# Shifting the split weight pieces of an fp32 transformer block off their 256-byte grid

## The chip, the cores and the metric

The kernel runs on one core of one Trainium2 chip, in one launch. The metric is device time in microseconds. The engines have the names of the profile: PE (TensorE: matmuls, with PEld for its weight loads), DVE (VectorE), ACT (ScalarE), POOL (GpSimd), SP (SyncE, which here only issues DMAs).

## What is computed

Two layers of a block with an attention and mLSTM mixer and a convolutional feed-forward part, on 512 positions of width 1024, all in fp32. Cut to what the change touches, which are the products with weights:

```python
D_MODEL, SEQ, DEPTH, D_FF = 1024, 512, 2, 2816

def hybrid_mixer(hn, w_in, ..., w_out):
    aq, ak, av, mq, mk, mv, mo, gates = jnp.split(hn @ w_in, split_at, axis=-1)   # 1024 x 3600
    ...                                     # dilated attention, mLSTM in both directions
    return jnp.concatenate([attn, mlstm], axis=-1) @ w_out                        # 1024 x 1024

def conv_ffn(hn, w_up, conv_w, conv_b, w_down):
    u = depthwise_conv_centred(hn @ w_up, conv_w, conv_b)                         # 1024 x 5632
    gate, val = jnp.split(u, 2, axis=-1)
    return (jax.nn.gelu(gate, approximate=True) * val) @ w_down                   # 2816 x 1024

def reference(x, ...):
    for l in range(DEPTH):
        mixed = hybrid_mixer(rms_norm(x, mix_pre_g[l]), w_in[l], ..., w_out[l])
        x = x + rms_norm(mixed, mix_post_g[l])
        ff = conv_ffn(rms_norm(x, ffn_pre_g[l]), w_up[l], ffn_conv_w[l], ffn_conv_b[l], w_down[l])
        x = x + rms_norm(ff, ffn_post_g[l])
    return x
```

## The kernel before

Activations lie with features on the 128 partitions and the 512 positions along the row. To keep fp32 accuracy on PE, each fp32 operand is split into a high part in PE's fp32r format and the rest, also in fp32r; a product is then three matmuls that add up in PSUM: high weight by high activation (line 224), low weight by high activation (225), high weight by low activation (226). The helper `mac` issues these three for one block of 128 features.

The weights stream from HBM in 208 pieces in a fixed order (`plan`): per layer 28 of w_in, 8 of w_out, 44 of w_up and 24 of w_down. A piece has up to 8 blocks of 128x128, 4096 bytes a partition. `load_raw` brings a piece into one of three buffers `wraw`. `split_w` makes the two parts: ACT copies it to fp32r into `whi` (line 177), and DVE subtracts that from the raw piece into `wlo` (line 115, in `lo_part`). `whi` and `wlo` have three buffers each (RING), so pieces are split ahead, by `prefetch`, as soon as PE has finished with a buffer. 192 of the 208 pieces go there. The other 16 are put by `alloc` into space that other tiles have left (names `wsp`, `wnx`, `wlh`, `wll`, and some `pth`, `ptl`).

For most products a block of a piece is the stationary operand of a matmul and the activation streams past it, 512 columns at a time, or 256 at the edges of a stage. A full piece is then 24 matmuls of 512 columns. In the V projections (two pieces for each of four head groups and layer, lines 920 to 922) it is the other way round: the activation is stationary and 256 columns of a piece stream. In `first_group` and at the start of w_out several pieces are used in turn, block by block. The attention and mLSTM work of the mixer is issued between the steps of its projections, so small matmuls stand among the large ones there; in the feed-forward part, after its first group, hardly anything does.

All tiles of a partition's memory come from a wrapper, `Lines`, that rounds sizes up to 256 bytes; tiles under that size go to a pool of their own. So every large tile begins at a multiple of 256 bytes, and so do the blocks of a piece, 512 bytes each. An exception is in the borrowed space of w_out's third output tile, whose low parts lie in rows of 129 numbers (516 bytes), because the tiles `cs0` and `cs1` whose space it takes are so shaped:

```python
spare = [("kw0", "cs0", 3, 1), ("kw1", "cs1", 3, 1), ("lu", "ut", 1, 2), ("lu", "uu", 1, 2)]
...
w = P + 1 if t[0] == "c" else P
ts.append(mp.tile([P, n * w], F32R, tag=t, ...).rearrange("p (n m) -> p n m", n=n)[:, :, 0:P])
```

The first three blocks of that piece are in kw0 and cs0, the next three in kw1 and cs1. Another is the table tb, whose parts begin 56 bytes behind a multiple of 256.

Of the kernel before, what the change touches and what calls it, by code (L numbers as in the profile page):

```python
# [9 lines left out]
F32R = mybir.dt.float32r  # L10
# [6 lines left out]
P = 128  # L17
# [64 lines left out]
def tile_hybrid_block(ctx: ExitStack, tc: tile.TileContext, xt, w_in, w_g, w_out, w_up, w_down, par, cst, out):  # L82
# [8 lines left out]
    wraw_p, whi_p, wlo_p = Lines(big, small, RAW), Lines(big, small, RING), Lines(big, small, RING)  # L91
# [22 lines left out]
    def lo_part(dst, src, hi):  # L114
        nc.vector.tensor_tensor(out=dst, in0=src, in1=f32v(hi), op=ALU.subtract)  # L115
# [34 lines left out]
    nxt = [0, 0]  # L150

    def load_raw():
        i = nxt[0]
        if i >= len(plan):
            return
        nxt[0] += 1
        nk = plan[i].shape[1]
        raw = wraw_p.tile([P, 8, P], F32, tag="wraw", name="wraw")
        nc.sync.dma_start(out=raw[:, 0:nk, :], in_=plan[i])
        raw_q.append((raw, nk))  # L160

    def split_w(alloc=None):

        if not raw_q:
            return None
        raw, nk = raw_q.popleft()
        parts = {}
        n = 8
        k = 0
        while k < nk:  # L170
            if alloc is None:
                hi = whi_p.tile([P, 8, P], F32R, tag="whi", name="whi")
                lo = wlo_p.tile([P, 8, P], F32R, tag="wlo", name="wlo")
            else:
                hi, lo, n = alloc()
            m = min(n, nk - k)
            nc.scalar.copy(out=hi[:, 0:m, :], in_=raw[:, k:k + m, :])  # L177
            lo_part(lo[:, 0:m, :], raw[:, k:k + m, :], hi[:, 0:m, :])
            for j in range(m):
                parts[k + j] = (hi[:, j, :], lo[:, j, :])  # L180
            parts["all"] = (hi, lo)
            k += m
        load_raw()
        return parts
# [11 lines left out]
    def take():  # L196
        return ready.popleft() if ready else split_w()

    def prefetch(n):
        while len(ready) < n and raw_q:  # L200
            ready.append(split_w())
# [303 lines left out]
    def mixer(l, xp, first, mp, post):  # L505
# [488 lines left out]
        for n, k in enumerate(order[:7]):  # L994
            for w, ps in zip(ws, pss):
                mac(ps, w, k, cp[k], n == 0, False)
            A.run(2)
            if n == 2:
                ready.append(split_w(spare_place))
# [279 lines left out]
```

## Time and profile before

| | before |
|---|---|
| median of the runs | 1360.45 us (1360.37 to 1360.54, 2 runs) |
| the profiled execution | 1360.24 us |
| its span, first to last instruction | 1358.5 us |
| mean granted TensorE clock | 0.997 |
| PE busy | 1323.6 us, 7152 matmuls |
| PE weight loads | 1128.5 us, 7152, beside the matmuls |
| DVE busy | 955.5 us, 1885 instructions |
| ACT busy | 719.6 us, 1226 instructions |
| DMA | 115.34 MB, 85 GB/s on average |

Rows of groups read: line, engine, operation, out<-in tiles, shape, count | busy us, mean ns of one | idle us of the engine before them, and what ended it. Rows of a timeline read: start us, duration us, engine, line, operation, tiles, shape. Successive matmuls overlap in the profile, since one is drawn from its first read to its last result; the distance from one start to the next is the rate at which PE takes them.

### The profile page before, as it was taken

How to read it: one execution, taken by the hardware profiler on the slowest of the kernel's cores; microseconds unless marked ns; L12 is line 12 of the kernel's file. 1: busy time of each engine (PE TensorE's matmuls, PEld its weight loads, DVE VectorE, ACT ScalarE, POOL GpSimd, SP SyncE). 2: the span in 40 equal slices, each digit the busy share in tenths (PEclk: the TensorE clock that was granted, in tenths of full speed). 3: DMA queues.
4: the chain of work that ended last, by engine and by line, in shares of the span. 5: the costliest groups of instructions: out<-in, count | busy, mean ns of one | idle time of the engine just before them, and what ended most of it. 6: DMA issues, size and time to landing. Idle time of an engine off the chain costs nothing. (4 is left out here: it accounts for less than half of the span.)

```text
span 1358.5 us, 18690 instructions
## 1 busy us (share of the span) xinstructions
PE 1323.6 (97%) x7152; PEld 1128.5 (83%) x7152; DVE 955.5 (70%) x1885; ACT 719.6 (53%) x1226; POOL 109.6 (8%) x116
## 2 busy tenths in 40 slices
PE   7999999999999999999989999999999999999997
PEld 6788878889888888888977888888898888888886
DVE  6999887847887777422499998887469777773233
ACT  5596696654544444323346867966446444443230
POOL 0000100024000000001130001000330000000002
PEclk9999999999999999999999999999999999999998
DMA  6212112241233332333322222122313333333321
GB/s 236 64 48 79 34 61 78 65 137 34 76 109 94 100 102 90 92 95 112 94 69 63 63 63 62 45 80 79 108 47 93 96 102 97 93 90 100 97 86 62
DMA packets 34089, 115.34 MB, mean 85 GB/s; under 512 B 3664, under 2 KB 6352, under 8 KB 34000
## 3 DMA queue, kind: packets, MB, share of 16 engines
q1 hardware_dynamic: 34000, 114.15, 27.6%
q8 instruction: 56, 0.92, 0.3%
q14 instruction: 33, 0.27, 0.1%
HBM read 112.04 MB, written 2.10 MB: 84 GB/s over the span
## 5 line engine op out<-in xcount | busy, mean ns | idle before, releaser
L115 DVE TENSOR_TENSOR wlo<-wraw,whi 128x1024 fp32r<-128x1024 f32 (+1 forms) x192 | 236.5, 1235 | 174.2 <-ACT whi L177 172.2
L224 PE MATMUL mm<-ah,whi 128*128 128x512 f32 (+1 forms) x880 | 335.9, 382 | 0.0
L225 PE MATMUL mm<-ah,wlo 128*128 128x512 f32 (+1 forms) x880 | 333.6, 379 | 0.0
L226 PE MATMUL mm<-al,whi 128*128 128x512 f32 (+1 forms) x880 | 332.2, 378 | 0.8 <-DVE al L372 0.8
L177 ACT CAST whi<-wraw 128x1024 fp32r<-128x1024 f32 (+1 forms) x192 | 197.8, 1035 | 162.2 <-PE mm L226 107.8
L226 PEld LDWEIGHTS mm<-al,whi 128*128 128x128 f32 x880 | 165.5, 188 | 30.7 <-DVE al L372 1.6
L224 PEld LDWEIGHTS mm<-ah,whi 128*128 128x128 f32 x880 | 166.1, 189 | 29.1 <-ACT whi L177 0.5
L225 PEld LDWEIGHTS mm<-ah,wlo 128*128 128x128 f32 x880 | 166.1, 189 | 27.6
L320 POOL TENSOR_TENSOR acc<-acc,sq 128x512 f32<-128x512 f32 x22 | 29.5, 1343 | 752.5 <-ACT sq L317 747.9
L224 PE MATMUL mm<-hh,whi 128*128 128x512 f32 x220 | 85.6, 389 | 0.0
L225 PE MATMUL mm<-hh,wlo 128*128 128x512 f32 x220 | 85.6, 389 | 0.0
L226 PE MATMUL mm<-hl,whi 128*128 128x512 f32 x220 | 85.6, 389 | 0.0
L1056 DVE TENSOR_TENSOR u<-mm,prow 128x512 f32<-128x512 f32 x64 | 43.8, 687 | 49.9 <-PE mm L226 39.5
L1073 ACT CAST hh<-cv 128x512 fp32r<-128x512 f32 x44 | 27.3, 620 | 87.6 <-DVE cv L1070 87.6
L920 PE MATMUL mm<-whi,ah 128*128 128x256 f32 x256 | 73.4, 288 | 0.2 <-DVE cu L658 0.2
L922 PE MATMUL mm<-whi,al 128*128 128x256 f32 x256 | 72.4, 283 | 0.0
L921 PE MATMUL mm<-wlo,ah 128*128 128x256 f32 x256 | 72.3, 283 | 0.0
L1068 ACT ACTIVATE cg<-cg 128x512 f32<-128x512 f32 x44 | 27.8, 633 | 74.7 <-DVE cg L1062 74.3
L225 PE MATMUL o<-ah,wlo 128*128 128x512 f32 (+1 forms) x160 | 60.6, 379 | 0.0
L224 PE MATMUL o<-ah,whi 128*128 128x512 f32 (+1 forms) x160 | 60.5, 378 | 0.0
L226 PE MATMUL o<-al,whi 128*128 128x512 f32 (+1 forms) x160 | 60.5, 378 | 0.0
L746 ACT ACTIVATE p<-p,mx 128x512 f32<-128x512 f32 x64 | 46.1, 721 | 17.9 <-DVE mx L743 17.9
(320 smaller groups left out, 2787.2 us busy)
## 6 DMA issues: line engine op xcount, KB each, us to landing
wraw<-in_w_up SPq DMA_DIRECT2D x88, 512.0 KB, 3.6
wraw<-in_w_in SPq DMA_DIRECT2D x56, 512.0 KB, 3.5
wraw<-in_w_down SPq DMA_DIRECT2D x32, 512.0 KB, 3.5
wraw<-in_w_out SPq DMA_DIRECT2D x16, 512.0 KB, 3.6
wraw<-in_w_down SPq DMA_DIRECT2D x16, 384.0 KB, 3.1
x<-in_xt SPq DMA_DIRECT2D x4, 512.0 KB, 6.7
out_dram<-x SPq DMA_DIRECT2D x8, 256.0 KB, 2.1
tb<-in_cst SPq DMA_DIRECT2D x2, 967.0 KB, 5.3
```

The source lines that it names most:

```text
L115: nc.vector.tensor_tensor(out=dst, in0=src, in1=f32v(hi), op=ALU.subtract)
L177: nc.scalar.copy(out=hi[:, 0:m, :], in_=raw[:, k:k + m, :])
L224: nc.tensor.matmul(out=ps, lhsT=hi, rhs=rh, start=first, stop=False)
L225: nc.tensor.matmul(out=ps, lhsT=lo, rhs=rh, start=False, stop=False)
L226: clock[1] = nc.tensor.matmul(out=ps, lhsT=hi, rhs=rl, start=False, stop=last).ins
L320: e.tensor_tensor(out=self.acc[:, cols], in0=self.acc[:, cols], in1=sq, op=ALU.add)
L746: nc.scalar.activation(out=p_, in_=p_, func=AF.Exp, scale=-1.0, bias=mx, accum_out=den)
L920: nc.tensor.matmul(out=o_, lhsT=xh, rhs=hi, start=(k == 0), stop=False)
L921: nc.tensor.matmul(out=o_, lhsT=xh, rhs=lo, start=False, stop=False)
L922: clock[1] = nc.tensor.matmul(out=o_, lhsT=xl, rhs=hi, start=False, stop=(k == KT - 1)).ins
L1056: nc.vector.tensor_tensor(out=u, in0=ps, in1=st["row"], op=ALU.mult)
L1068: nc.scalar.activation(out=g, in_=g, func=AF.Gelu_apprx_tanh)
```

## The change

The tiles of the ring become 256 bytes longer (1088 instead of 1024 numbers). A counter of split pieces gives each piece a distance from its tile's start: 0, 2, 4, ... 62 numbers, that is 0, 8, 16, ... 248 bytes, then 0 again. `hi` and `lo` of one piece have the same distance. Pieces in borrowed space, the raw pieces and all activations stay at multiples of 256. Because six tiles grow by 256 bytes, what lies behind them moves up by at most 1536 bytes, in steps of 256.

```diff
@@ -169,8 +169,10 @@
         k = 0
         while k < nk:
             if alloc is None:
-                hi = whi_p.tile([P, 8, P], F32R, tag="whi", name="whi")
-                lo = wlo_p.tile([P, 8, P], F32R, tag="wlo", name="wlo")
+                o = 2 * (nxt[1] % 32)
+                nxt[1] += 1
+                hi, lo = (q.tile([P, 8 * P + 64], F32R, tag=t, name=t)[:, o:o + 8 * P].rearrange("p (k c) -> p k c", k=8)
+                          for q, t in ((whi_p, "whi"), (wlo_p, "wlo")))
             else:
                 hi, lo, n = alloc()
             m = min(n, nk - k)
```

Every engine has the same instructions in the same order with the same waits as before; the kernel's lines behind the edit have numbers higher by two.

## The prediction

> **What bounds the kernel now.** I read the page first (busy shares, slices, chain, costliest groups), then the groups with shapes kept apart, then stretches of the timeline for TensorE alone.
>
> ```profile
> span 1358.5 us, 18690 instructions
> PE 1323.6 (97%) x7152; PEld 1128.5 (83%) x7152; DVE 955.5 (70%) x1885; ACT 719.6 (53%) x1226; POOL 109.6 (8%) x116
> PE   7999999999999999999989999999999999999997
> PEclk9999999999999999999999999999999999999998
> L115 DVE TENSOR_TENSOR wlo<-wraw,whi 128x1024 fp32r<-128x1024 f32 (+1 forms) x192 | 236.5, 1235 | 174.2 <-ACT whi L177 172.2
> L177 ACT CAST whi<-wraw 128x1024 fp32r<-128x1024 f32 (+1 forms) x192 | 197.8, 1035 | 162.2 <-PE mm L226 107.8
> ```
>
> PE (matrix multiplies) is busy 97% of the span, at nearly the full clock in every slice. The two instructions that make a split piece are slaves of PE: the cast on ACT (L177) idles 162.2 us in all, most of it until a matmul of L226 has let go of a ring buffer, and the subtraction on DVE (L115) idles for the cast. So nothing feeds PE late, and the time is the number of matmuls by their cadence. The cadence is read from the distance of starts, since the ends are modelled. A stretch of 260 us in each layer's feed-forward part has nothing but matmuls of 512 columns:
>
> ```profile
> 380.00:640.00 260.00, 260.00 (x1149) 215.29 (x1148) 152.06 (x183) 102.41 (x128) 5.17 (x4) 1.00 0.32 96
> 1040.00:1300.00 260.00, 260.00 (x1149) 215.29 (x1148) 160.27 (x196) 105.41 (x132) 3.88 (x3) 1.00 0.33 97
> 419.78 0.39 PE L224 MATMUL mm<-ah,whi 128*128 128x512 f32 x1
> ...
> 421.82 0.39 PE L224 MATMUL o<-ah,whi 128*128 128x512 f32 x1
> ```
>
> The columns of the first two rows are the window, its length, and the busy time and count of PE, weight load, DVE, ACT and POOL. 1149 matmuls in 260.00 us are 226.3 ns each (the two at the edges are cut); the two starts with nine matmuls between them give 2.04 / 9 = 226.7 ns. Both layers show the same count, so this cadence holds without exception while DVE is busy 58% and ACT 39% of the same stretch.
>
> **The change, part by part.** Every instruction, its order and its waits stay; only addresses change. 192 pieces (x192 above) get tiles 256 bytes longer, and piece i begins 8 x (i mod 32) bytes into its tile, with hi and lo of one piece at the same distance. Six of the 192 stay at zero, 96 are at a multiple of 16, 96 at an odd multiple of 8. Four kinds of work touch these addresses.
>
> *DVE's subtraction.* Its neighbours show operands at unequal distances already:
>
> ```profile
> L704 DVE TENSOR_TENSOR ra<-ra,rb 128x512 f32<-128x512 f32 x16 | 14.7, 920 | 0.1
> L703 DVE TENSOR_TENSOR rb<-rb,tb 128x512 f32<-128x512 f32 x16 | 10.9, 682 | 0.0
> L1070 DVE TENSOR_TENSOR cv<-cv,cg 128x512 f32<-128x512 f32 x44 | 30.4, 690 | 1.1
> L1060 DVE SCALAR_TENSOR_TENSOR cv<-u,par,cv 128x511 f32<-128x511 f32 x44 | 32.8, 746 | 2.2 <-ACT cv L1059 2.2
> L372 DVE SCALAR_TENSOR_TENSOR al<-x,par,ah 128x512 fp32r<-128x512 f32 x8 | 5.6, 747 | 3.0 <-ACT ah L371 3.0
> ```
>
> L703 reads a part of tb that begins 56 bytes behind a multiple of 256 and takes 682 ns; L1070, all aligned, takes 690. L1060 reads and writes 4 bytes off and takes 746; L372, all aligned, 747. I cost this part at 0.
>
> *ACT's cast* writes off the line. No row has ACT writing so. The nearest rows are DVE's above (0 ns); as the other end I take the largest gap between like operations there, 920 against 682 ns (L704 against L703, both of 512 numbers), so 0.24 us a cast. Both are hidden: a piece is split two pieces ahead, 2 x 24 matmuls x 0.2267 = 10.9 us, and cast plus subtraction take 1.04 + 1.24 = 2.3 us. Without that cover it would be 192 x 0.24 = 46 us; I take 0.
>
> *The weight load* is the part that matters, since pieces are the stationary operand of most matmuls. One place of the trace has stationary operands off the line: the third output tile of w_out takes its piece from borrowed buffers (tile wsp), whose low halves lie in rows of 129 numbers, so that blocks 1 and 4 begin 4 bytes and blocks 2 and 5 8 bytes behind a multiple of 256. The load itself does not show it:
>
> ```profile
> L225 PEld LDWEIGHTS o<-cp,wsp x16: 187/188/189, 275.8 to 952.8; 128*128 128x128 f32 x16
> ```
>
> (duration in ns: least, median, most, the displaced ones among them). But the matmuls around these loads do. Blocks come in the order 0, 1, 2, 4, 5, 6, 7, 3:
>
> ```profile
> 276.06 0.39 PE L225 MATMUL o<-cp,wsp 128*128 128x512 f32 x1
> 276.29 0.39 PE L226 MATMUL o<-cp,wsp 128*128 128x512 f32 x1
> 276.51 0.40 PE L224 MATMUL o<-cp,wsp 128*128 128x512 f32 x1
> ...
> 279.53 0.39 PE L225 MATMUL o<-cp,wsp 128*128 128x512 f32 x1
> ...
> 281.79 0.39 PE L226 MATMUL mm<-cp,whi 128*128 128x512 f32 x1
> ```
>
> From 276.51 (block 1) to 279.53 (block 6) thirteen matmuls take 3.02 us, 232.3 ns each; the ten from there to 281.79, all with aligned operands, take 2.26 us, 226 each. So four displaced loads among aligned ones throw PE out of its even cadence at +5.6 ns a matmul, 0.073 us in all (3.02 - 13 x 0.2267), and it falls back at once. The same state comes after any foreign instruction between aligned matmuls:
>
> ```profile
> 266.74 0.60 PE L882 MATMUL t<-c,hs 128*128 128x128 f32 x4
> 267.09 0.48 PE L225 MATMUL mm<-cp,wlo 128*128 128x512 f32 x1
> 267.41 0.39 PE L226 MATMUL mm<-cp,whi 128*128 128x512 f32 x1
> ...
> 268.57 0.39 PE L225 MATMUL mm<-cp,wlo 128*128 128x512 f32 x1
> ...
> 269.25 0.39 PE L225 MATMUL mm<-cp,wlo 128*128 128x512 f32 x1
> ```
>
> After four transposes, five matmuls take 1.16 us (232 each), the next three 0.68 (226.7). One such hunt costs 1.16 - 5 x 0.2267 = 0.027 us, and PE then finds its cadence again. In the changed kernel the distance is the same for all 24 matmuls of a piece and steps at its edge. I therefore expect one hunt at each edge, not a lasting loss: in the feed-forward parts 2 x (40 + 21) = 122 pieces, and about half of the other 54 stationary pieces, which stand among foreign work and hunt already in part: 149 x 0.027 = 4.0 us. The ends for this term: 0 (the step of 8 bytes is too small to disturb), and +5.6 ns on every matmul that has such a piece stationary:
>
> ```profile
> L224 PE MATMUL mm<-ah,whi 128*128 128x512 f32 x768 | 304.0, 396 | 0.0
> L224 PE MATMUL mm<-hh,whi 128*128 128x512 f32 x220 | 85.6, 389 | 0.0
> L224 PE MATMUL o<-ah,whi 128*128 128x512 f32 x144 | 56.0, 389 | 0.0
> L224 PE MATMUL o<-hh,whi 128*128 128x512 f32 x88 | 34.2, 389 | 0.0
> L224 PE MATMUL mm<-cp,whi 128*128 128x512 f32 x80 | 31.2, 395 | 0.0
> ```
>
> These are 1300 of L224, so 3900 with L225 and L226: 3900 x 5.6 ns = 22 us.
>
> *The streamed read.* In the V projections (16 pieces, L920 to L922) the piece is the streaming operand, 256 columns at a time.
>
> ```profile
> L920 PE MATMUL mm<-whi,ah 128*128 128x256 f32 x256 | 73.4, 288 | 0.2 <-DVE cu L658 0.2
> 699.07 0.28 PE L921 MATMUL mm<-wlo,ah 128*128 128x256 f32 x1
> ...
> 699.66 0.28 PE L920 MATMUL mm<-whi,ah 128*128 128x256 f32 x1
> ...
> 700.26 0.28 PE L922 MATMUL mm<-whi,al 128*128 128x256 f32 x1
> ```
>
> Here the hunt is shorter, not longer: five matmuls in 0.59 us (118 ns), then five in 0.60 (120). With 768 such matmuls and some 370 of 256 columns with a piece stationary, losing the cadence gives back at most 1140 x 2 ns = 2.3 us. I take 0, and -2.3 as the lower end. The reverse, a displaced stream read at the 5.6 ns of above, would be 768 x 5.6 = 4.3 us.
>
> The sum: the profiled execution took 1360.24 us (1358.5 of span and 1.74 around it; the median of the runs is 1360.45). 1360.24 + 0 + 0 + 4.0 + 0 = 1364.2, so 1364.
>
> Two rules bear on the weight load. The Trainium skill's page "SBUF — State Buffer", section "Specifications (TRN2)", gives SBUF lines of 16 bytes and says that each crossing to a new line pays. By it a block of 128 numbers at an odd multiple of 8 bytes touches 33 lines instead of 32, at a multiple of 16 still 32, so half of the pieces would pay, and the sum would be that of rival 2 below. The displaced loads of the trace (187 to 189 ns) do not show it in their own duration; the matmuls around them may. The page "TensorE: Matmul & The Clock Gate", section "Step-by-step: what each phase is for", gives TensorE two independent read ports and says that loading the next weights takes nothing from the running matmul; by it the sum would be 1360. The 232.3 ns around wsp speak against it, unless something else than the loads disturbs there.
>
> **The rivals.**
> 1. *It does nothing that can be seen*: the addresses of one piece agree among themselves, and the cadence does not feel a step of 8 bytes. For it: hi, lo and moving tiles in the feed-forward part lie at many different multiples of 256 and the count of 1149 does not care. 1360.
> 2. *Half of the pieces lose the cadence for good*, those at odd multiples of 8. 3900 / 2 x 5.6 ns = 10.9 us: 1371. For it: both distances in wsp (4 and 8) are off a multiple of 16; against it: they stood between aligned loads, so a change and a distance can't be told apart there.
> 3. *All displaced pieces lose it*: 22 us less the 256-column gain, 1360.2 + 22 - 2 = 1380; with only the 2844 feed-forward matmuls (3 x (640 + 308)) still at the even cadence to lose, 16 us: 1376. I take 1378.
> 4. *Each displaced load costs by itself*, which ends on the slow side: the 0.073 us around wsp belong to four loads, 18 ns each, and the fall back after the last one is as quick as a price by load would make it. All three loads of a step are displaced now, so 3900 x 18 ns x 31/32 = 68 us: 1428. It decides from 7 ns a load on (27 us, 2%). Against it: the hunt after the transposes reaches the same 232 ns with no displaced load, so 5.6 ns looks like the price of the state.
> 5. *The equal distance is what costs now*: 512 columns take 226.7 and 256 columns 120 ns, so 256 columns more cost 106.7 and 13.3 ns a matmul are fixed. If these come from stationary and stream meeting at equal distances, and go, 3900 x 13.3 = 52 us: 1308. Against it: no stretch of the trace with unequal distances runs 512 columns faster than 226.
>
> **How the numbers follow.** Forecast (hunts at the edges, 1364) 0.38; rival 1 (1360) 0.14; rival 2 (1371) 0.14; rival 3 (1378) 0.18; rival 4 (1428) 0.12; rival 5 (1308) 0.04. The range 1357 to 1384 takes in the forecast and the first three rivals (0.84), with the -2.3 us below and, above, rival 3 at its full 1380 and the 4.3 us of a displaced stream. Beyond 2%, which is about what a measurement of this kernel can tell from no change, lie only rival 4 (slower, 0.12) and rival 5 (faster, 0.04); within are 0.84.
>
> **What would show it.** In the two feed-forward windows the count of PE shows each case: 1149 for rival 1, about 1144 for the forecast (some 45 edges x 0.027 = 1.2 us in 260), 1134 for rival 2, 1120 for rival 3, 1063 for rival 4, over 1200 for rival 5. In the timeline the forecast wants some five starts 232 ns apart after a piece's edge and 226.7 in the rest; rival 3 wants no even stretch. The groups of L115 should stay at 1235 and of L177 near 1035 ns; if L177 grows, that step was wrong, and if PE's weight load then waits for whi or wlo, the cover was too. The prediction fails if displacement acts on a load by its distance and not by the step from load to load.

## The result, and the profile after

| | before | after |
|---|---|---|
| median of the runs | 1360.45 us | 1376.64 us (1376.49 to 1376.79, 2 runs) |
| span of the profiled execution | 1358.5 us | 1374.8 us |
| mean granted TensorE clock | 0.997 | 0.996 |

The time after is 1.0122 times the time before, 95% interval 1.0104 to 1.0141: 16.2 us more, within the predicted range, but by rival 3 and not by the forecast.

The page of the changed kernel, with the lines that answer to those shown of before:

```profile
span 1374.8 us, 18690 instructions
PE 1342.3 (98%) x7152; PEld 1130.4 (82%) x7152; DVE 956.1 (70%) x1885; ACT 716.5 (52%) x1226; POOL 109.5 (8%) x116
PE   7999999999999999999989999999999999999997
PEclk9999999999999999999999999999999999999999
L115 DVE TENSOR_TENSOR wlo<-wraw,whi 128x1024 fp32r<-128x1024 f32 (+1 forms) x192 | 236.7, 1235 | 182.0 <-ACT whi L179 181.3
L179 ACT CAST whi<-wraw 128x1024 fp32r<-128x1024 f32 (+1 forms) x192 | 197.3, 1032 | 177.0 <-PE mm L228 119.1
```

PE is busy 18.7 us longer (1323.6 to 1342.3) with the same 7152 matmuls at the same clock. DVE's subtraction takes 1235 ns as before and ACT's cast 1032 (1035 before), both with displaced outputs. The cast idles longer (177.0 against 162.2 us), and what ends its waits is still a matmul: the pieces come early enough, PE takes them more slowly. The two feed-forward windows (columns as in the prediction; the second lies 10 us later, as the layer does):

```profile
380.00:640.00 260.00, 260.00 (x1122) 210.51 (x1121) 151.31 (x183) 99.52 (x126) 5.19 (x4) 1.00 0.31 93
1050.00:1310.00 260.00, 260.00 (x1122) 210.50 (x1121) 158.55 (x194) 101.37 (x128) 3.89 (x3) 1.00 0.32 94
```

1122 matmuls in place of 1149: 231.7 ns each in place of 226.3. Where the 16 us lie in the program is seen from the first and last starts of a tile's matmuls. These rows give line, operation, count, duration (least, median, most, ns), first and last start in us and shape; the first three are of before, the others of after:

```profile
L224 PE MATMUL t<-ah,wnx x16: 389/396/486, 333.3 to 1011.1; 128*128 128x512 f32 x16
L224 PE MATMUL o<-hh,whi x88: 389/389/389, 552.4 to 1313.6; 128*128 128x512 f32 x88
L224 PE MATMUL mm<-hh,wlh x66: 278/283/365, 657.1 to 1346.4; 128*128 128x256 f32 x66
```
```profile
L226 PE MATMUL t<-ah,wnx x16: 389/395/486, 333.9 to 1019.9; 128*128 128x512 f32 x16
L226 PE MATMUL o<-hh,whi x88: 389/394/404, 558.1 to 1329.6; 128*128 128x512 f32 x88
L226 PE MATMUL mm<-hh,wlh x66: 278/283/365, 665.3 to 1362.8; 128*128 128x256 f32 x66
```

The wnx matmuls of 512 columns stand at the beginning of each feed-forward part, behind its first group; the first wlh matmul comes near the first part's end. Against before, the starts are late by 0.6 us at 333.9, 5.7 at 558.1, 8.2 at 665.3, 8.8 at 1019.9 and 16.4 at 1362.8. So each feed-forward part loses 7.6 us and each mixer 0.6.

Within the feed-forward part, the loss differs from piece to piece, and not at the edges. Here are the first matmuls of three successive pieces of after, which begin 120, 128 and 136 bytes behind a multiple of 256 (start, duration, both in us):

```profile
402.34 0.39 PE L226 MATMUL o<-ah,whi 128*128 128x512 f32 x1
...
407.79 0.40 PE L226 MATMUL mm<-ah,whi 128*128 128x512 f32 x1
...
413.38 0.40 PE L226 MATMUL mm<-ah,whi 128*128 128x512 f32 x1
```

The 24 matmuls of the piece at 120 bytes take 5.45 us, 227 ns each, which is the old cadence; the 24 of the piece at 128 take 5.59 us, 233 each, and not one of its groups of three takes less than 690 ns, where three at the old cadence take 680.

Below, a *step* is the three matmuls of one block (L224 to L226 of before), 3 x 226.7 = 680 ns in the even cadence. Mean lengths of a step in the feed-forward parts of after, from the starts in the trace, by the distance of the piece (of the pieces that no other matmul interrupts):

| length of a step | distances (bytes) |
|---|---|
| 680 to 685 ns | 0, 120, 240 |
| 687 to 697 ns | 8, 24, 80, 152, 176, 184, 192, 200, 208, 216, 232 |
| 698 to 703 ns | 16, 32 to 72, 88 to 112, 128 to 144, 160, 168, 224, 248 |

### The profile page after: what moved, and what is told of

Same layout as the page of the kernel before. It is cut to its first block, busy times and chain, and to the rows that moved or that the text cites. A ratio compares the mean times of both kernels' runs of the same rounds, so it can differ in the third digit from the quotient of the medians.

```text
span 1374.8 us, 18690 instructions
## 1 busy us (share of the span) xinstructions
PE 1342.3 (98%) x7152; PEld 1130.4 (82%) x7152; DVE 956.1 (70%) x1885; ACT 716.5 (52%) x1226; POOL 109.5 (8%) x116
## 5 line engine op out<-in xcount | busy, mean ns | idle before, releaser
L115 DVE TENSOR_TENSOR wlo<-wraw,whi 128x1024 fp32r<-128x1024 f32 (+1 forms) x192 | 236.7, 1235 | 182.0 <-ACT whi L179 181.3
L226 PE MATMUL mm<-ah,whi 128*128 128x512 f32 (+1 forms) x880 | 339.9, 387 | 0.0
L227 PE MATMUL mm<-ah,wlo 128*128 128x512 f32 (+1 forms) x880 | 337.1, 383 | 0.0
L228 PE MATMUL mm<-al,whi 128*128 128x512 f32 (+1 forms) x880 | 335.8, 383 | 0.9 <-DVE al L374 0.9
L179 ACT CAST whi<-wraw 128x1024 fp32r<-128x1024 f32 (+1 forms) x192 | 197.3, 1032 | 177.0 <-PE mm L228 119.1
L226 PEld LDWEIGHTS mm<-ah,whi 128*128 128x128 f32 x880 | 166.7, 189 | 32.5 <-ACT whi L179 0.5
L226 PE MATMUL mm<-hh,whi 128*128 128x512 f32 x220 | 86.6, 394 | 0.0
L226 PE MATMUL o<-ah,whi 128*128 128x512 f32 (+1 forms) x160 | 61.3, 383 | 0.0
```

Of the source, the lines that this page charges most:

```text
L226: nc.tensor.matmul(out=ps, lhsT=hi, rhs=rh, start=first, stop=False)
L227: nc.tensor.matmul(out=ps, lhsT=lo, rhs=rh, start=False, stop=False)
L228: clock[1] = nc.tensor.matmul(out=ps, lhsT=hi, rhs=rl, start=False, stop=last).ins
```

## The experiments

Theories on the table: **hunts**, the forecast (PE loses its cadence when the distance steps, for about five matmuls); **distance** (each distance has a cadence of its own, as long as it lasts); and, within the second, distance from what: of the weights from a multiple of 256, or from the activation that streams past them. Diffs are against after where they change `o` or the pieces' line, and against before in the two that change a filler (an unused tile that moves what lies behind it). Ratios are to the kernel before in runs on the same chip, with 95% intervals. The row below each is its first feed-forward window (columns as above).

**Longer tiles and steps of whole 256 bytes.**

```diff
-                o = 2 * (nxt[1] % 32)
+                o = 64 * (nxt[1] % 2)
```

> The ring's tiles are as long as in the change, and pieces begin in turn 0 and 256 bytes behind their tile's start, so every block stays at a multiple of 256. If the distance of the stationary operand modulo 256 is what breaks the even cadence, this is the kernel before again: 1149 matmuls in the two feed-forward windows of 260 us, 226.7 ns from start to start, about 1360.5 us. If longer tiles, the tiles that move up behind them, or the mere alternation of places cost, it comes near the change: about 1122 matmuls and 1377 us.

1360.04 us, ratio 0.9999 (0.9990 to 1.0009).

```profile
380.00:640.00 260.00, 260.00 (x1149) 215.38 (x1148) 152.01 (x184) 102.45 (x127) 5.17 (x4) 1.00 0.33 96
```

The larger tiles and a step of 256 bytes at each piece cost nothing. What costs is the part below 256.

**The same 8 bytes for every piece.**

```diff
-                o = 2 * (nxt[1] % 32)
+                o = 2
```

> Every piece begins 8 bytes behind a multiple of 256; there is no step from piece to piece. My forecast (a hunt at each edge where the distance changes) gives the cadence back: 226.7 ns, 1149 matmuls in a feed-forward window, about 1361 us. The theory by distance says that each distance has a cadence of its own, and in the changed kernel's trace the feed-forward pieces at 8 run at 231.0 ns: some 1126 matmuls in a window, and with some 3300 matmuls of 512 columns 4.3 ns longer 14 us more, about 1375 us.

1372.45 us, ratio 1.0088 (1.0072 to 1.0105).

```profile
380.00:640.00 260.00, 260.00 (x1128) 211.75 (x1128) 151.31 (x183) 99.89 (x126) 5.18 (x4) 1.00 0.32 94
```

From piece to piece nothing steps here, so there is no edge to hunt at, and three quarters of the loss is still there (12.2 of 16.2 us). This is the run that takes the forecast's mechanism away. 260 / 1128 = 230.5 ns agrees with the pieces at 8 bytes in after (steps of 692 ns, 692 / 3 = 230.7).

**The same 120 bytes for every piece.**

```diff
-                o = 2 * (nxt[1] % 32)
+                o = 30
```

> Every piece begins 120 bytes behind a multiple of 256. In the changed kernel's trace the feed-forward pieces at 120 were the only displaced ones at the even cadence, 226.7 ns with nothing after the first matmul. The theory by distance: 1149 matmuls in a feed-forward window and about 1361 us, though every piece is displaced. If every start off the grid (or off a line of 16 or 64 bytes, which 120 is too) costs and those pieces were an accident of their neighbours, about 231 to 233 ns, 1115 to 1126 matmuls and 1375 to 1382 us.

1360.42 us, ratio 1.0002 (0.9992 to 1.0011).

```profile
380.00:640.00 260.00, 260.00 (x1148) 215.29 (x1148) 152.03 (x183) 102.30 (x127) 5.15 (x4) 1.00 0.33 96
```

The distance that costs nothing in after costs nothing alone. 120 is an odd multiple of 8, so being off a 16-byte line is not the cause.

**64 bytes for every piece.**

```diff
-                o = 2 * (nxt[1] % 32)
+                o = 16
```

> Every piece, high and low, begins 64 bytes behind a multiple of 256; the activations stay. By the distance, each feed-forward matmul takes the 233.3 ns that the changed kernel's pieces at 64 show: 1114 matmuls in a window of 260 us, 3300 x 6.6 ns = 22 us, about 1382 us, slower than the change though no distance ever steps. If a distance that is a multiple of 64 bytes (or of 16) were harmless and the neighbours' odd ones had done it, 1149 matmuls and 1360.5 us.

1380.02 us, ratio 1.0142 (1.0127 to 1.0158).

```profile
380.00:640.00 260.00, 260.00 (x1116) 209.50 (x1115) 151.13 (x182) 99.12 (x125) 5.19 (x4) 1.00 0.31 92
```

A multiple of 64 costs more than 8 bytes. In the trace, starts are 231 and 236 ns apart in turn, mean 233.3.

**Everything by 64 bytes**: a longer filler ahead of the large tiles, on before, moves weights and activations alike.

```diff
-    big.tile([P, 32], F32, name="fill")
+    big.tile([P, 48], F32, name="fill")
```

> The kernel before with its first filler tile 64 bytes longer, so that every tile of memory, pieces and activations alike, begins 64 bytes behind a multiple of 256. If only the distance between the stationary and the streaming operand counts, it is the kernel before: 226.7 ns, 1149 matmuls in a feed-forward window, about 1360.5 us. If the absolute place of the stationary operand counts, the cadence is that of the change's pieces at 64, 233.4 ns: 1114 matmuls, 3300 x 6.7 ns = 22 us more, about 1382 us.

1360.67 us, ratio 1.0003 (0.9993 to 1.0012).

```profile
380.00:640.00 260.00, 260.00 (x1149) 215.29 (x1148) 151.59 (x183) 102.40 (x128) 5.16 (x4) 1.00 0.32 96
```

64 bytes for the weights alone cost 19.8 us; 64 bytes for both cost nothing. So it isn't the place of the weights by itself that matters but their distance from the activation, as far as this one common shift shows.

**The activations by 64 bytes, weights in place**: a filler ahead of the feed-forward tiles, on before. The input of the up-projection (ah, al) lies elsewhere and stays; hh and hl, the streams of the down-projection, move.

```diff
+            fb.tile([P, 16], F32, name="fillf")
             fp = Lines(fb, fb)
```

> The kernel before with a filler of 64 bytes at the head of the feed-forward tiles: the activations that stream in the down projection (hh, hl) begin 64 bytes behind a multiple of 256, every weight piece stays on it, and the up projection has its tiles as before. If the distance is that of the stationary operand from the stream, it is -64, that is 192, and the down projection's 924 matmuls of 512 columns run at the changed kernel's 229.0 to 229.3 ns for 192: +2 us, about 1362.6. If only the size of the distance counts, they run at its 233.3 ns for 64: +6 us, about 1366.5. If the stream's place has no part in it, they stay at 226.7 ns and the time at 1360.4.

1362.36 us, ratio 1.0014 (1.0005 to 1.0023). A window of the down-projection, first in before, then here:

```profile
590.00:650.00 60.00, 60.00 (x266) 49.70 (x265) 17.90 (x18) 18.60 (x26) 5.17 (x4) 1.00 0.38 113
```
```profile
590.00:650.00 60.00, 60.00 (x264) 49.23 (x263) 18.21 (x18) 17.93 (x25) 5.18 (x4) 1.00 0.37 107
```

Displaced activations cost too, though not as much as weights at 64: 264 matmuls, where the weights at 64 leave 259 in the same window:

```profile
590.00:650.00 60.00, 60.00 (x259) 48.35 (x258) 15.97 (x13) 16.88 (x22) 5.19 (x4) 1.00 0.32 94
```

The same size of distance, two prices: the sign might count, weights less stream, with -64 the same as 192 modulo 256. The next run was made for that.

**192 bytes for every piece.**

```diff
-                o = 2 * (nxt[1] % 32)
+                o = 48
```

> All ring pieces 192 bytes behind multiples of 256, all activations at 0. In an earlier run the streams hh and hl of the down-projection began 64 bytes off and the pieces at 0, and its starts there repeated 232, 226, 229 ns, mean 228.9; with the pieces at 64 and the streams at 0 they alternated 231 and 236, mean 233.3. If what counts is the signed distance, stationary less stream modulo 256, then 192 here is that earlier case (0 - 64 = -64 = 192): starts of 232, 226 and 229 in the down-projection, mean 228.9, the same now in the up-projection, about 1136 matmuls in each feed-forward window of 260 us (260 / 0.2289), and 2844 x 2.2 ns = 6 us more than before, 1367 us. If only the size of the distance counts (192 is 64 away from the next multiple): as the run with the pieces at 64, 1116 a window and 1380 us. If it is a property of the displaced side: starts of its own kind, neither of the two patterns.

1365.76 us, ratio 1.0042 (1.0025 to 1.0059). The windows, feed-forward and down-projection:

```profile
380.00:640.00 260.00, 260.00 (x1138) 213.53 (x1137) 150.47 (x181) 99.54 (x125) 5.20 (x4) 1.00 0.32 96
590.00:650.00 60.00, 60.00 (x264) 49.25 (x263) 18.90 (x18) 18.05 (x26) 5.20 (x4) 1.00 0.35 104
```

1138 where the signed distance gave 1136 and the unsigned one 1116. The distances of starts in the down-projection, means by line over some 308 starts each, in ns, show it more sharply:

| weights less stream | after the high by high matmul | after the low by high | after the high by low | mean |
|---|---|---|---|---|
| 0 (before) | 226.5 | 227.0 | 226.5 | 226.7 |
| 0 - 64 = 192 (activations moved) | 231.7 | 225.9 | 229.2 | 228.9 |
| 192 (weights moved) | 225.8 | 229.1 | 231.7 | 228.9 |
| 64 (weights moved) | 233.5 | 233.2 | 233.3 | 233.3 |

The same three values come back, in a cycle that begins at another matmul of the step. Moving the activations by 64 is the same as moving the weights by 192, and not the same as moving them by 64.

**Only the low weights displaced**, by 64 bytes.

```diff
-                o = 2 * (nxt[1] % 32)
-                nxt[1] += 1
                 ...
-                          for q, t in ((whi_p, "whi"), (wlo_p, "wlo")))
+                          for q, t, o in ((whi_p, "whi", 0), (wlo_p, "wlo", 16)))
```

> Only the low parts begin 64 bytes behind a multiple of 256, so one load of three is displaced. If each load has its own price (the load of the low block runs beside the first matmul of a step), one matmul of three takes 233.3 ns and two 226.7: 228.9 ns on average, 1136 in a window, about 1367.5 us. If one displaced load throws the whole step out, as the four loads of wsp seemed to in the kernel before, all three take 230 to 233 ns: 1114 to 1130 in a window and 1371 to 1382 us.

1373.91 us, ratio 1.0097 (1.0083 to 1.0111).

```profile
380.00:640.00 260.00, 260.00 (x1127) 211.31 (x1126) 150.78 (x183) 99.77 (x126) 5.17 (x4) 1.00 0.32 94
```

Every third load is displaced, and two thirds of the loss of all three is there (13.7 of 19.8 us). The starts in a step are 229.2, 235.8 and 228.3 ns apart, 693.3 in all: the longest follows the start of the matmul with the displaced weights, but the two behind the aligned ones are longer than 226.7 too. Of the two cases foreseen it is the second, in which one displaced load throws the whole step out. The price does not add up by loads: 13 ns a step for one displaced load of three, 20 for three.

**Two sweeps**, one run each, to find a distance that is faster than 0 for 512 columns. First all pieces 4 bytes further than in after (4, 12, ... 252), then only the low parts at after's distances.

```diff
-                o = 2 * (nxt[1] % 32)
+                o = 2 * (nxt[1] % 32) + 1
```

> The change with every distance 4 bytes larger: 4, 12, 20, ... 252, a new one for each piece, high and low alike. It gives the cadence of 32 more distances in one run. The theory by distance: again one repeating pattern for each distance in the feed-forward part, between 226.7 and 234 ns, the same whenever the distance comes again, and about 1376 us like the change (no distance is zero now, so perhaps 1 us more). If 4 bytes off the earlier distances matters by itself (odd multiples of the 4-byte number being worse), every distance at 233 ns or more and 1383 us or over. A distance under 226 ns would point to a faster kernel.

```diff
-                hi, lo = (q.tile(...)[:, o:o + 8 * P].rearrange("p (k c) -> p k c", k=8)
-                          for q, t in ((whi_p, "whi"), (wlo_p, "wlo")))
+                hi, lo = (q.tile(...)[:, d:d + 8 * P].rearrange("p (k c) -> p k c", k=8)
+                          for q, t, d in ((whi_p, "whi", 0), (wlo_p, "wlo", o)))
```

> The high parts stay on the grid and the low parts begin 0, 8, ... 248 bytes behind it, another distance for each piece. It shows whether the two parts at unequal distances can run below the even cadence. By e7, where 64 bytes for the low part gave 229.2, 235.8 and 228.3 ns for the three matmuls of a step, the theory is a pattern by distance with sums of three from 680 to 700 ns, and about 1372 to 1376 us. A sum under 678 ns at some distance would point to a faster kernel; if only the low load paid, sums would never exceed 687.

1379.99 and 1374.06 us, against 1360.05 of before beside them. The mean step of a distance took 680 ns (100 bytes) to 711 (164 bytes) in the first, and in the second 680 (0), 682 (120), 684 (240), and 689 to 706 for all others. The first run is slower than the 1376 us foreseen and two of its distances, 164 and 212, go beyond the 234 ns foreseen, to 237 and 236 a matmul. It also has two more distances that cost next to nothing, 100 bytes (680 ns) and 156 (681), neither of them a multiple of 8. No distance tried has a mean step under 680, so for 512 columns 226.7 ns is the floor as far as these 64 distances show.

**Displacement only where 256 columns stream.** There the sweep had shown distances under the old 120 ns. The V projections' pieces go to 112 bytes, the pieces of the 256-wide groups at the head of the feed-forward parts and of layer 1's mixer to 8, all others to 0.

```diff
-                o = 2 * (nxt[1] % 32)
-                nxt[1] += 1
+                i = nxt[0] - len(raw_q) - 1
+                m = i % 104
+                o = 28 if m in (2, 3, 10, 11, 14, 15, 22, 23) else 2 if 36 <= m < 40 or i in (104, 105) else 0
```

> A trial of a better kernel. Pieces stay on the grid where 512 columns stream, and are displaced only where 256 do: the V projections' pieces, which are the stream there, by 112 bytes (117.3 ns in the changed kernel against 120 before), and the pieces of the first feed-forward group and of the second layer's first mixer group by 8 bytes (117.1 against 120). If the loss of the cadence is a gain for 256 columns, some 610 x 2.7 + 270 x 2.9 ns = 2.4 us less than before, about 1358.0 us. If waits of these stages take it back, 1360.4 us. The feed-forward windows stay at 1149.

1358.14 us, ratio 0.9984 (0.9975 to 0.9993): 0.16% faster than before, and faster than after. The feed-forward window is that of before, and the groups of the V projection are shorter (288, 283 and 283 ns in before):

```profile
380.00:640.00 260.00, 260.00 (x1149) 215.29 (x1148) 152.25 (x183) 101.97 (x127) 5.17 (x4) 1.00 0.33 96
L923 PE MATMUL mm<-whi,ah 128*128 128x256 f32 x256 | 72.2, 283 | 0.3 <-DVE cu L661 0.3
L925 PE MATMUL mm<-whi,al 128*128 128x256 f32 x256 | 71.0, 278 | 0.0
769.62 0.28 PE L924 MATMUL mm<-wlo,ah 128*128 128x256 f32 x1
...
773.13 0.28 PE L925 MATMUL mm<-whi,al 128*128 128x256 f32 x1
```

The last two rows have 31 distances between them: 3.51 / 31 = 113.2 ns in place of 120. Over the V matmuls that follow each other without a wait the mean is 114.9 (119.5 before), since each stretch needs a while to settle; behind the first eight starts, all six long stretches are at 113.3 to 113.5. In the groups at 8 bytes the mean is 116.8 (119.6).

**The same with the second kind of group at 144 bytes.** In the V projections the activation is stationary and the piece streams, so that the distance of the stationary operand from the stream is 0 - 112 = 144 modulo 256. If the signed distance is all that counts, pieces held still at 144 should show the same 113 ns.

```diff
-                o = 28 if m in (2, 3, 10, 11, 14, 15, 22, 23) else 2 if 36 <= m < 40 or i in (104, 105) else 0
+                o = 28 if m in (2, 3, 10, 11, 14, 15, 22, 23) else 36 if 36 <= m < 40 or i in (104, 105) else 0
```

> The kernel with pieces only behind the 256-column groups, of which the stationary pieces (the groups that hold the streamed weights still) begin 144 bytes behind multiples of 256 in place of 8; the streamed pieces of the V projections stay at 112, all others at 0. Signed distance (stationary less stream, modulo 256): 144 in both kinds of group now, since 0 - 112 = 144. So these groups' 768 matmuls should show the start distances that the V projections showed, about 113.3 ns once settled, in place of about 116.5 ns in the 256-wide stationary groups of the run before: near 1 to 1.5 us less than that run, 1357 us, against 1360.4 of the kernel before the change. Unsigned distance, or a property of the streamed side alone: the stationary groups at 144 behave as their own class, start distances anywhere between 113 and 120 ns and not those of V; time 1358 to 1361.

1358.64 us, ratio 0.9986 (0.9977 to 0.9995). The intervals of this run and the one before can't be told apart, but the starts can: 119.1 ns in these groups (mean), in place of 116.8 with 8 bytes and 113 as foreseen. So here the rule of the signed distance failed. What differs besides is that two matmuls in a row have the same stationary part in the V projections (lines 923 and 924 here), and that several pieces are used in turn here; whether one of these is the reason was not tried. The trace of the run with 192 bytes for every piece warns of more: there the V projections stream from one distance throughout, yet four of their six long stretches settle at 113.3 to 113.4 ns and two at 117.8, in both layers alike. The two at 117.8 begin right behind a matmul of 512 columns, the four behind another V matmul and a break (some 200 ns from start to start). So for 256 columns a distance alone does not fix the cadence, and the rule of the signed distance is not shown to hold there; for 512 columns it is shown for the distances 64 and 192.

## Why the prediction was right or wrong

**The bound** held. PE was 98% busy, no feeding engine came late, and the loss is the number of matmuls by their cadence: over the 2838 pairs of successive 512-column starts in the feed-forward parts the sum of distances went from 643.9 to 659.0 us, 15.1 of the 16.2.

**DVE's subtraction and ACT's cast** at 0 held: 1235 ns and 1032 ns. The other end of the cast, 0.24 us each, was not seen.

**The weight load** is the step that failed, at "I therefore expect one hunt at each edge, not a lasting loss". It was put at 4.0 us and measured about 16. The rows around wsp were right and their meaning was not: I saw 232 ns there and 232 ns after the transposes, took both for one state that PE falls into and leaves, and so made a displaced load a disturbance. The first starts (L224) of blocks 1, 2, 4, 5 and 6 in before, of which the first four are displaced, show what wsp was:

```profile
276.51 0.40 PE L224 MATMUL o<-cp,wsp 128*128 128x512 f32 x1
...
277.21 0.39 PE L224 MATMUL o<-cp,wsp 128*128 128x512 f32 x1
...
277.90 0.39 PE L224 MATMUL o<-cp,wsp 128*128 128x512 f32 x1
...
278.60 0.40 PE L224 MATMUL o<-cp,wsp 128*128 128x512 f32 x1
...
279.30 0.39 PE L224 MATMUL o<-cp,wsp 128*128 128x512 f32 x1
```

In the nanoseconds of the trace, the steps of the four displaced blocks take 696, 693, 700 and 694, which is 63 ns over 4 x 680; the one right behind them takes 684, and the ones before and after that 680. So nearly all of what I had put down to a hunt (73 ns from rounded starts, 67 from those in nanoseconds) is paid in the displaced steps themselves. The sweep of the low parts gives the same size: one low load of three displaced by 8 bytes makes a step 693 ns. That PE went back to its cadence is then no recovery: the displaced blocks had ended. The hunt after the transposes is another thing: there all operands are aligned. The last sentence of the prediction names the case: displacement acts by its distance, not by the step from load to load.

**The streamed read** at 0 held as a sum: the 732 distances between successive V matmuls add up to 89.8 us before and 89.7 after. Single distances move it, though: one that was chosen for it, with that of the first groups, gives back some 2 us.

**Rival 1** (nothing) and **rival 2** (odd multiples of 8) fell: 16, 32, 64 and 128 bytes cost about as much as the dearest in after (698 to 700 ns a step), and 120 nothing. So the 16-byte lines in "SBUF — State Buffer" of the Trainium skill ("Specifications (TRN2)") don't order these prices. **Rival 4** (18 ns for each displaced load) fell with 1122 matmuls in a window where it gave 1063; three displaced loads of a step cost 20 ns together at 64 bytes, not 54. **Rival 5** fell: no distance tried is faster than the equal one for 512 columns; for 256 a little of it is true (113 against 120).

**Rival 3** (all displaced pieces lose it) is what happened: 1122 matmuls a window where it gave 1120, and 1376.6 us where it gave 1378. Its upper end of 22 us counted 3900 matmuls, which was too many: foreign matmuls stand among those of the mixers, where the 961 pairs of successive starts went from a mean of 236.4 to 239.4 ns, 3.0 each and 2.9 us in all, and by the rows above other distances gave back more than half of that (0.6 us a mixer was left). The lower end, 16 us from the feed-forward matmuls alone, was the better count. It should have had 2796 of them, since 48 of the 2844 have a piece in borrowed space (wnx), which stays aligned; that is 0.3 us. And not all displaced pieces pay: those at 120 bytes don't, and those at 240 hardly.

**The number** was within the range by its width and not by the forecast: the forecast's one cost, 4.0 us, is a quarter of what was measured, and the upper end had been drawn to take in rival 3.

The other page cited, "TensorE: Matmul & The Clock Gate" of the Trainium skill ("Step-by-step: what each phase is for"), says that loading the next tile's weights "doesn't steal SBUF read bandwidth from the running matmul". No run here looks at the reads themselves, but as a rule for the rate, as the prediction used it, it did not hold: moving the weights alone by 64 bytes takes 512-column matmuls from 226.7 to 233.3 ns. The load's own duration hardly shows it, 189 ns on average before and after:

```profile
L226 PEld LDWEIGHTS mm<-ah,whi 128*128 128x128 f32 x880 | 166.7, 189 | 32.5 <-ACT whi L179 0.5 <-issue 0.3
```

## What to carry to other kernels

When a kernel is bound as this one is, by back-to-back fp32r matmuls of 512 columns with a weight load each, give weights and activations the same distance from a multiple of 256 bytes. Judge any move of a tile by the distance of matmul starts: the load durations hardly show it, and PE is busy for 260.00 of 260.00 us in the window either way. When a trace shows a small loss in a rare place, find out whether it ends because the engine recovers or because its cause ends, before multiplying it by a count: the first makes it a price per event, the second a price per instruction. A number of matmuls in a fixed window (1149, 1138, 1122, 1116) resolved these cases to one matmul in a thousand.

## What the hardware showed that was not expected

- The rate of 512-column fp32r matmuls depends on the distance of the stationary from the streaming operand, modulo 256 bytes: 226.7 ns at 0, 226.7 to 226.8 at 100, 120 and 156, 228.9 at 192, 230.7 at 8, 233.3 at 64, 237 at 164. That the sign of the distance counts is shown for 64 against 192. Neither the size of the distance nor lines of 16 or 64 bytes order it.
- At 64 bytes starts are 231 and 236 ns apart in turn, at 192 bytes 226, 229 and 232, for as long as the distance lasts. The four distances that were run by themselves have the steps there that they have in after: 692 ns and 692 at 8, 700 and 700 at 64, 680 and 680 at 120, 687 and 687 at 192.
- For 256 columns the aligned 120 ns is not the least: with the stream 112 bytes behind a multiple of 256 and the stationary operand at one, starts settle at 113.2 to 113.5 ns. One distance can have two cadences there (113.3 and 117.8 ns with the stream 192 bytes behind); what decides between the two was not tried.
- What in PE or in its reads of SBUF makes the cycle stays open. The runs fix what it depends on, not how it comes about.
